# Weight remainders made by Pool instead of Vector during an expert sort, and a third buffer for stored activations

## Chip, cores and metric

The kernel runs on one core of a Trainium2 chip. The metric is the device time of one execution in microseconds; the median of the runs is given. The engines are called by the names of the profile: PE (TensorE matmul), PEld (its weight loads), DVE (VectorE), ACT (ScalarE), POOL (GpSimd) and SP (SyncE, which here only issues transfers). A name with a q behind it (SPq, ACTq) is the engine's queue, where its transfers are issued.

## What is computed

Two transformer-like blocks on 512 tokens of width 1024, all in float32: an SSD and gated-linear-attention mixer, a latent-attention layer, two gated feed-forward layers, an HGRN2 and retention mixer, and last a PEER layer (product-key experts), then a final norm. The change is in the PEER layer, with one exception at the very end:

```python
def peer_ffn(h, w_q, sub_keys, expert_u, expert_v):
    q = (ht @ w_q).reshape(T, 8, 2, 128)
    s = jnp.einsum('thpd,hpkd->thpk', q, sub_keys) 
    top_s, top_i = lax.top_k(s, 16)
    cand = top_s[:, :, 0, :, None] + top_s[:, :, 1, None, :]
    best_s, best_c = lax.top_k(cand.reshape(T, 8, 256), 16)
    ...
    gates = jax.nn.softmax(best_s, axis=-1)
    act = jax.nn.gelu(jnp.einsum('td,thkd->thk', xb, expert_u[expert_idx]))
    return jnp.einsum('thk,thkd->td', gates * act, expert_v[expert_idx])
```

## The kernel before

**Products.** A float32 matmul is made of three in a faster format: each operand is split into a high part (ACT casts it, `whi` for weights) and a remainder (`lo = src - hi`, `wlo`), and `mm3` adds hi x hi, hi x lo and lo x hi in PSUM. The weights come as a fixed stream of blocks of 128 x 1024 (0.524 MB each). `weight(name)` hands out the next block and first sees to it that the blocks behind it are loaded (`_issue`, on SP's queue) and split (`_prep`, which calls `split`, line 329). The remainder is made on DVE at line 334, like all other remainders. In the PEER layer there are four buffers each for the raw block, `whi` and `wlo`.

**The PEER layer** treats its four token tiles in two ways. For the first three tiles (384 tokens) all 16384 experts are computed densely: u blocks (128 experts each, `u`, 24 matmuls of 384 columns) give activations, v blocks (`v`, 18 matmuls of 512 columns) add weighted rows of `expert_v` into six PSUM banks. For the last tile the 128 chosen rows of `expert_u` and of `expert_v` for each token are gathered from DRAM by indirect transfers on POOL (`fetch`, line 1659, six row buffers) and treated on DVE (lines 1671 and 1678); this is the generator `rows`.

The order in time is:

1. 16 blocks of `w_pq` (queries), each followed by the scores against the keys; then u blocks 0 to 71, whose activations are stored to DRAM (`ad`, in pairs, lines 1477 and 1479). This is `main`. Into it the generator `side` is woven: first the sort of the scores (`topk`, `top16` from line 1685, on DVE alone) for eight heads, then the softmax (`soft`), then eight empty steps, then `gates`, which builds for the three dense tiles the gate of every expert by one-hot products (lines 1772 to 1790) and writes them to DRAM (`gd`, line 1756). `rows` is woven in beside it. How many steps of `side` and of `rows` are made per block of `main` is set by the numbers around line 1529.
2. What is left of the u blocks, with rows at 0.5 a block.
3. 56 steps, n = 0 to 55, of a u block (72 to 127) and the v block of the same experts: `weigh` multiplies activations by gates (line 1582), which `load_g` has read back from `gd` (line 1558), and splits the product; `v_block` adds. 2.8 rows a step.
4. 72 steps with the v blocks 0 to 71, whose activations `load_a` reads back from `ad` (line 1562, two buffers of two blocks each); rows at a rate that finishes them three steps before the end. The last step adds the result into `x`, and `final` (line 1801) normalizes and writes out through tiles `fy`.

Each engine executes its instructions in the order that the framework's scheduler has given them, which is not always that of the source: loads whose buffers are free are moved up. The layer's normalized input is made tile by tile before it starts (`norm_scale`, half of each product on POOL at line 417), with one buffer `xn`, from which PE transposes it.

Of the kernel before, what the change touches and what calls it, by code (L numbers as in the profile page):

```python
# [139 lines left out]
class Net:  # L140
    def __init__(self, ctx, tc, ap, start=None):
        self.ctx, self.tc, self.nc, self.ap = ctx, tc, tc.nc, ap
        nc = self.nc
        pool = lambda name, bufs=1, **kw: ctx.enter_context(tc.tile_pool(name=name, bufs=bufs, **kw))
        self.cp = pool("cp")
        self.raw = pool("raw", 3)
        self.whi = pool("whi", 3)
        self.wlo = pool("wlo", 3)
        self.big = pool("big", 2)
        self.sm = pool("sm", 4)  # L150
        self.xd = pool("xdram", space=DRAM).tile([P, D], F32, name="xd")
        self.pacc = pool("pacc", 4, space=PSUM)
        self.psm = pool("psm", 4, space=PSUM)
        self.stream = stream_plan()
        self.wpos = 0
        self.wload = 0
        self.wready = 0
        self.wq = []
        self.more = None
        if start is not None:  # L160
            while self.stream[self.wpos][0] != start:
                self.wpos += 1
            self.wload = self.wready = self.wpos
        self.x = self.cp.tile([P, NT, D], F32, name="x")
        self.cst = self.cp.tile([P, NCST], F32, name="cst")
        self.vec = self.cp.tile([P, NVEC], F32, name="vec")
        self.ones = self.cp.tile([P, P], F32, name="ones")
        self.eps = self.cp.tile([P, 1], F32, name="eps")
        self.dummy = self.cp.tile([P, 1], F32, name="dummy")
        self.nwp = self.cp  # L170
        self.norm = 0
        self.sq = {}
        self.nT = None
        self.identb = self.cp.tile([P, P], BF16, name="identb")
        self.negb = self.cp.tile([P, 2, P], BF16, name="negb")
        self.id3 = self.cp.tile([P, 16], BF16, name="id3")
        nc.vector.memset(self.eps, EPS)
        nc.sync.dma_start(self.x[:, 0, :512], ap["x"][0:P, :512])
        nc.sync.dma_start(self.x[:, 0, 512:], ap["x"][0:P, 512:])
        self.load_norm()  # L180
        nc.sync.dma_start(self.x[:, 1], ap["x"][P:2 * P, :])
        nc.sync.dma_start(self.cst[:, :P], ap["cst"][:, :P])
        nc.sync.dma_start(self.x[:, 2], ap["x"][2 * P:3 * P, :])
        nc.sync.dma_start(self.x[:, 3], ap["x"][3 * P:4 * P, :])
        nc.scalar.activation(self.dummy, self.eps, AF.Sqrt)
        self.ident = self.c("ident")
        self._prep()
        self._prep()
# [41 lines left out]
    def _prep(self):  # L230
# [10 lines left out]
            return  # L241
        hi = self.wbuf(self.whi, self.wready).tile([P, WB], F32R, name="whi")
        lo = self.wbuf(self.wlo, self.wready).tile([P, WB], F32R, name="wlo")
        self.split(hi[:, :n], lo[:, :n], r[:, :n])
        self.wq[self.wready - self.wpos] = (hi, lo)
        self.wready += 1

# [78 lines left out]
                    if len(grp) == 2 or tt % 2:  # L326
                        yield

    def split(self, hi, lo, src, scale=None):

        nc = self.nc
        if scale is None:
            nc.scalar.copy(hi, src)  # L333
            nc.vector.tensor_tensor(lo, src, hi.bitcast(F32), ALU.subtract)  # L334
        else:
            nc.scalar.activation(hi, src, AF.Copy, scale=scale)
            nc.vector.scalar_tensor_tensor(lo, src, scale, hi.bitcast(F32), ALU.mult, ALU.subtract)
# [1108 lines left out]
    def peer(self, last=False):  # L1446
# [4 lines left out]
        with ExitStack() as es:  # L1451
# [5 lines left out]
            with ExitStack() as e1:  # L1457
# [63 lines left out]
                    nc.scalar.copy(sc[c].rearrange("p a b -> p (a b)"), p)  # L1521

                main = itertools.chain(self.formA("w_pq", 16, hh, hl, ev_q, lead=2), experts())
                next(main)
                acc = accr = 0.0
                fin = False
                for _ in main:
                    if self.heads < 9:
                        acc += 1.7
                        if self.heads:  # L1530
                            accr += 0.3
                    else:
                        acc += 1.3
                        accr += 0.5
                    while acc >= 1:
                        acc -= 1
                        if next(side, "end") == "end":
# [20 lines left out]
                        nc.sync.dma_start(g[:, a:b], gd[a:b, :, j * 32:(j + 8) * 32].rearrange("g p c -> p g c"))  # L1558

                def load_a(j):  # L1560
                    as_[j] = pv.tile([P, 2, TD], F32, name="a")
                    nc.sync.dma_start(as_[j], ad[j // 2])

                def u_block():
# [48 lines left out]

                load_g(0, 0, 4 * ND)
                for _ in main:
                    step(0.5)
                out = [[(self.accb if nb else self.smb)() for nb in range(2)] for tt in range(ND)]
                ups = [self.accb(), self.smb()]
                au = [u_block(), u_block()]
                for n in range(P - NS):  # L1620
                    w = weigh(n, au.pop(0))
                    if n + 2 < P - NS:
                        au.append(u_block())
                    if n + 4 - (P - NS) in (0, 2):
                        load_a(n + 4 - (P - NS))
                    v_block([n], [w])
                    step(2.8)
                rate = (2 * P - self.fetched) / (NS - 3)
                for n in range(P - NS, P):
                    j = order[n]  # L1630
                    w2 = weigh(n, as_[j - j % 2][:, j % 2])
                    if j % 2 and j + 3 < NS:
                        load_a(j + 3)
                    if n < P - 2:
                        v_block([n], [w2])
                        step(rate)
# [164 lines left out]
    def final(self, fp):  # L1801
# [4 lines left out]
        def tile_out(tt):  # L1806
            r = self.x_rstd(tt)
            for i in range(2):
                s = slice(i * 512, (i + 1) * 512)
                y = fp.tile([P, 512], F32, name="fy", bufs=3)  # L1810
                nc.vector.scalar_tensor_tensor(y, self.x[:, tt, s], r, fw[:, s], ALU.mult, ALU.mult)
                (nc.sync, nc.scalar)[i].dma_start(ap["y"][tt * P:(tt + 1) * P, s], y)

# [167 lines left out]
```

## Time and profile before

| | us |
|---|---|
| median of 3 runs | 3522.71 (3520.72 to 3525.72) |
| profiled execution | 3522.2 |
| its span, first to last instruction | 3520.4 |
| PE busy | 3453.3 |
| DVE busy | 2171.0 |
| POOL busy | 520.8 |

The granted clock of TensorE was 0.995 of full speed over the span. A group of instructions is shown as line, engine, operation, output and inputs by the program's names, shapes, count, busy time and mean duration; behind the bar stands the engine's idle time just before them and what ended it. In windows, each engine's busy time stands with its number of instructions, then the granted clock (1.00 is full speed), the mean busy share of the 16 DMA engines and the GB/s that they moved.

### The profile page before, as it was taken

How to read it: one execution, taken by the hardware profiler on the slowest of the kernel's cores; microseconds unless marked ns; L12 is line 12 of the kernel's file. 1: busy time of each engine (PE TensorE's matmuls, PEld its weight loads, DVE VectorE, ACT ScalarE, POOL GpSimd, SP SyncE). 2: the span in 40 equal slices, each digit the busy share in tenths (PEclk: the TensorE clock that was granted, in tenths of full speed). 3: DMA queues.
4: the chain of work that ended last, by engine and by line, in shares of the span. 5: the costliest groups of instructions: out<-in, count | busy, mean ns of one | idle time of the engine just before them, and what ended most of it. 6: DMA issues, size and time to landing. Idle time of an engine off the chain costs nothing.

```text
span 3520.4 us, 46078 instructions
## 1 busy us (share of the span) xinstructions
PE 3453.3 (98%) x17601; PEld 2934.9 (83%) x17601; DVE 2171.0 (62%) x4070; ACT 1363.4 (39%) x2246; POOL 520.8 (15%) x403
## 2 busy tenths in 40 slices
PE   8999999999999999999999999899999999999999
PEld 7887788888778888888888888789899999997887
DVE  4455643335753333488634343599998778888887
ACT  5345432225843222545323333333444333333333
POOL 1001100000000000122101000210111354443220
PEclk9999999999999999999999999999999999999999
DMA  3221222322113332312232222435688999999996
GB/s 134 72 90 66 72 90 96 100 92 79 47 37 96 96 97 95 100 66 63 85 117 81 87 90 91 142 122 168 220 311 305 335 334 323 328 335 335 342 353 213
DMA packets 178303, 555.12 MB, mean 158 GB/s; under 512 B 19169, under 2 KB 44897, under 8 KB 177954
## 3 DMA queue, kind: packets, MB, share of 16 engines
q1 hardware_dynamic: 122944, 365.94, 31.0%
q0 software_dynamic: 36864, 134.23, 10.8%
q10 hardware_dynamic: 18274, 52.00, 3.9%
q8 instruction: 138, 2.26, 0.3%
q14 instruction: 83, 0.68, 0.1%
HBM read 508.07 MB, written 44.04 MB: 157 GB/s over the span
## 4 chain that ended last, share of the span: by engine, by line
PE 88%; DVE 7%; DMA 2%; ACT 1%; issue 1%; POOL 1%; SPq 0%; ACTq 0%; POOLq 0%; DVEq 0%
PE acc L262 22%; PE acc L263 22%; PE acc L264 22%; PE smb L264 4%; PE smb L263 4%; PE smb L262 4%; DVE wlo L334 1%; PE smb L1307 1%; PE smb L1028 1%; DMA a<-ad 1%; PE acc L996 1%; PE smb L1787 1%; PE smb L1788 1%; PE smb L1016 1%; PE smb L1424 0%
## 5 line engine op out<-in xcount | busy, mean ns | idle before, releaser
L334 DVE TENSOR_TENSOR wlo<-raw,whi 128x1024 fp32r<-128x1024 f32 (+2 forms) x621 | 761.0, 1227 | 653.2 <-ACT whi L333 629.0
L333 ACT CAST whi<-raw 128x1024 fp32r<-128x1024 f32 (+2 forms) x621 | 644.4, 1040 | 1258.1 <-PE acc L263 567.9
L264 PE MATMUL acc<-big_hi,wlo 128*128 128x512 f32 (+2 forms) x2504 | 918.1, 367 | 8.0 <-DVE wlo L334 7.7
L262 PE MATMUL acc<-big_hi,whi 128*128 128x512 f32 (+2 forms) x2504 | 923.0, 369 | 0.7 <-ACT big_hi L333 0.4
L263 PE MATMUL acc<-big_lo,whi 128*128 128x512 f32 (+2 forms) x2504 | 918.6, 367 | 1.2 <-DVE big_lo L334 1.1
L264 PEld LDWEIGHTS acc<-big_hi,wlo 128*128 128x128 f32 x2504 | 474.9, 190 | 72.2 <-DVE wlo L334 13.2
L262 PEld LDWEIGHTS acc<-big_hi,whi 128*128 128x128 f32 x2504 | 475.1, 190 | 61.8 <-ACT big_hi L333 1.0
L263 PEld LDWEIGHTS acc<-big_lo,whi 128*128 128x128 f32 x2504 | 475.5, 190 | 60.5 <-DVE big_lo L334 2.1
L262 PE MATMUL acc<-whi,big_hi 128*128 128x512 f32 x768 | 311.6, 406 | 2.3 <-DVE yret L1198 1.5
L263 PE MATMUL acc<-wlo,big_hi 128*128 128x512 f32 x768 | 300.9, 392 | 0.9 <-DVE wlo L334 0.9
L264 PE MATMUL acc<-whi,big_lo 128*128 128x512 f32 x768 | 301.6, 393 | 0.0
L1659 POOL DMA_INDIRECT row<-u_rows,ix x128 | 185.8, 1451 | 559.0 <-DVE row L1671 463.2
L1659 POOL DMA_INDIRECT row<-v,ix x128 | 153.9, 1203 | 295.5 <-DVE x L1678 272.5
L417 POOL TENSOR_TENSOR xn<-x,nw 128x512 f32<-128x512 f32 x24 | 35.2, 1469 | 1060.2 <-DVE x L458 1010.2
L333 ACT CAST wh<-w 128x384 fp32r<-128x384 f32 x128 | 65.6, 513 | 323.7 <-issue 164.7
L262 PEld LDWEIGHTS acc<-whi,big_hi 128*128 128x128 f32 x768 | 144.6, 188 | 35.2 <-issue 2.5
L263 PEld LDWEIGHTS acc<-wlo,big_hi 128*128 128x128 f32 x768 | 144.7, 188 | 30.9 <-issue 1.9
L264 PEld LDWEIGHTS acc<-whi,big_lo 128*128 128x128 f32 x768 | 144.4, 188 | 30.1
L1678 DVE SCALAR_TENSOR_TENSOR x<-row,act,x 128x1024 f32<-128x1024 f32 x128 | 164.0, 1282 | 1.3
L264 PE MATMUL smb<-whi,wl 128*128 128x512 f32 x384 | 150.9, 393 | 6.0 <-DVE wl L334 6.0
L1671 DVE SCALAR_TENSOR_TENSOR row<-row,xr 128x1024 f32<-128x1024 f32 x128 | 151.6, 1220 | 0.0
L263 PE MATMUL smb<-wlo,wh 128*128 128x512 f32 x384 | 150.4, 392 | 0.0
(525 smaller groups left out, 5363.6 us busy)
## 6 DMA issues: line engine op xcount, KB each, us to landing
raw<-u SPq DMA_DIRECT2D x128, 512.0 KB, 5.6
raw<-v SPq DMA_DIRECT2D x128, 512.0 KB, 5.9
raw<-w_gu SPq DMA_DIRECT2D x88, 512.0 KB, 3.5
raw<-w_dn SPq DMA_DIRECT2D x40, 512.0 KB, 3.6
ad<-pa ACTq DMA_DIRECT2D x36, 384.0 KB, 5.1
a<-ad SPq DMA_DIRECT2D x36, 384.0 KB, 5.4
gd<-big_hi ACTq DMA_DIRECT2D x24, 512.0 KB, 6.0
gd<-big_lo ACTq DMA_DIRECT2D x24, 512.0 KB, 6.1
```

What stands on the lines that cost most here:

```text
L262: mm(out, lh, rh, start=start, stop=False)
L263: mm(out, lh, rl, start=False, stop=False)
L264: mm(out, ll, rh, start=False, stop=stop)
L333: nc.scalar.copy(hi, src)
L334: nc.vector.tensor_tensor(lo, src, hi.bitcast(F32), ALU.subtract)
L996: mm(p[:, :n - P], q[:, i * P:n], k[:, :n - P], start=True, stop=True)
L1016: nc.tensor.transpose(banks[b][:, o + (i - k) * P:o + (i - k + 1) * P], es[i][:, k * P:(k + 1) * P], self.ident)
L1028: mm(po[64 * e:64 * e + 64, k * P:], vn[:, k, h + e], ts[e][k][:, :T - k * P], start=(k == 0), stop=(k == NT - 1))
L1307: mm(pa[:, tt - i], kx[:, tt], qx[:, tt], start=True, stop=True)
L1659: nc.gpsimd.indirect_dma_start(out=g, out_offset=None, in_=src, in_offset=bass.IndirectOffsetOnAxis(ap=ix[:, i, k:k + 1], axis=0))
L1671: pin(v.scalar_tensor_tensor(g, g, 1.0, xn, ALU.mult, ALU.mult, accum_out=act[:, k:k + 1]))
L1678: pin(v.scalar_tensor_tensor(x, g, act[:, k:k + 1], x, ALU.mult, ALU.add))
```

## The change

Between the PEER layer's first product and the end of the softmax, the remainders of weight blocks are made on POOL instead of DVE; no rows are fetched in that time, and 1.5 steps of the sort are asked for per block in place of 1.7. After it, rows are taken at 0.4 a block instead of 0.5 while the gates are made, and at 1.5 a block after them. The tile for stored activations has three buffers instead of two, and its loads are issued two blocks earlier; the output tile `fy` has two instead of three.

```diff
@@ __init__
+        self.sub = self.nc.vector
@@ _prep
-        self.split(hi[:, :n], lo[:, :n], r[:, :n])
+        self.split(hi[:, :n], lo[:, :n], r[:, :n], sub=self.sub)
@@ split
-    def split(self, hi, lo, src, scale=None):
+    def split(self, hi, lo, src, scale=None, sub=None):
...
             nc.scalar.copy(hi, src)
-            nc.vector.tensor_tensor(lo, src, hi.bitcast(F32), ALU.subtract)
+            (sub or nc.vector).tensor_tensor(lo, src, hi.bitcast(F32), ALU.subtract)
@@ peer
                 main = itertools.chain(self.formA("w_pq", 16, hh, hl, ev_q, lead=2), experts())
+                self.sub = nc.gpsimd
                 next(main)
                 acc = accr = 0.0
                 fin = False
                 for _ in main:
+                    if self.heads == 9:
+                        self.sub = nc.vector
                     if self.heads < 9:
-                        acc += 1.7
-                        if self.heads:
-                            accr += 0.3
+                        acc += 1.5
                     else:
                         acc += 1.3
-                        accr += 0.5
+                        accr += 0.4
...
                 def load_a(j):
-                    as_[j] = pv.tile([P, 2, TD], F32, name="a")
+                    as_[j] = pv.tile([P, 2, TD], F32, name="a", bufs=3)
                     nc.sync.dma_start(as_[j], ad[j // 2])
...
                 load_g(0, 0, 4 * ND)
                 for _ in main:
-                    step(0.5)
+                    step(1.5)
...
-                    if n + 4 - (P - NS) in (0, 2):
-                        load_a(n + 4 - (P - NS))
+                    if n + 8 - (P - NS) in (0, 2, 4):
+                        load_a(n + 8 - (P - NS))
...
-                    if j % 2 and j + 3 < NS:
-                        load_a(j + 3)
+                    if j % 2 and j + 5 < NS:
+                        load_a(j + 5)
@@ final
-                y = fp.tile([P, 512], F32, name="fy", bufs=3)
+                y = fp.tile([P, 512], F32, name="fy", bufs=2)
```

The order of instructions on three engines shows where things now stand (line numbers of the changed program are one or two higher).

POOL, from the end of the mixer into the PEER layer, before (`mt` belongs to the mixer, `xn` to the input's norm):

```order
L1169 TENSOR_TENSOR kr<-kr,rt 128x512
L1244 TENSOR_TENSOR mt<-mt,yret 128x512 x8
L417 TENSOR_TENSOR xn<-x,nw 128x512 x4
L1659 DMA row<-u_rows,ix 128x1024 x128
L1659 DMA row<-v,ix 128x1024 x128
```

and now:

```order
L1245 TENSOR_TENSOR mt<-mt,yret 128x512 x8
L335 TENSOR_TENSOR wlo<-raw,whi 128x1024
L418 TENSOR_TENSOR xn<-x,nw 128x512 x2
L335 TENSOR_TENSOR wlo<-raw,whi 128x1024
L418 TENSOR_TENSOR xn<-x,nw 128x512
L335 TENSOR_TENSOR wlo<-raw,whi 128x1024
L418 TENSOR_TENSOR xn<-x,nw 128x512
L335 TENSOR_TENSOR wlo<-raw,whi 128x1024 x4
L1661 DMA row<-u_rows,ix 128x1024 x2
L335 TENSOR_TENSOR wlo<-raw,whi 128x1024
L1661 DMA row<-u_rows,ix 128x1024 x4
L335 TENSOR_TENSOR wlo<-raw,whi 128x1024 x39
```

47 remainders stand on POOL, three of them ahead of an `xn`, and the first six row fetches stand between them.

ACT, at the end of the gates, before (`COPY big_lo` takes the last gates out of PSUM, `gd` is their write to DRAM, `pa` the activations of a u block that is stored, `af` those of a u block that is used at once):

```order
L1790 COPY big_lo<-smb 128x128x4
L1756 DMA gd<-big_lo 128x1024 x4
L1477 ACTIVATE pa<-acc 128x384 x2
L333 CAST whi<-raw 128x1024
L1479 DMA ad_16896<-pa 128x768
L333 CAST whi<-raw 128x1024
L1477 ACTIVATE pa<-acc 128x384
L1674 ACTIVATE act<-act 128x16
L333 CAST whi<-raw 128x1024 x2
L1477 ACTIVATE pa<-acc 128x384
L1479 DMA ad_16897<-pa 128x768
```

and now:

```order
L1792 COPY big_lo<-smb 128x128x4 x2
L1758 DMA gd<-big_lo 128x1024 x4
L1478 ACTIVATE pa<-acc 128x384
L334 CAST whi<-raw 128x1024
L1480 DMA ad_16898<-pa 128x768
L1574 ACTIVATE af<-acc 128x384
L334 CAST whi<-raw 128x1024 x2
L1574 ACTIVATE af<-smb 128x384
L334 CAST wh<-w 128x384
L334 CAST whi<-raw 128x1024
L1574 ACTIVATE af<-acc 128x384
```

Six `pa` followed the last gate write before the first `af` (four of them are shown); now one does. On PE, 216 matmuls of u blocks stood between the last gate product and the first product of a v block, and now 98.

SP, the loads around the same place, before (`a` is a pair of stored activations, `big_hi` and `big_lo` receive gates of eight blocks each):

```order
L226 DMA raw<-u 128x1024 x72
L1562 DMA a<-ad_16863 128x768
L226 DMA raw<-u 128x1024 x2
L1562 DMA a<-ad_16864 128x768
L1558 DMA big_lo<-gd 128x2x256 x4
L1558 DMA big_hi<-gd 128x12x256
L226 DMA raw<-u 128x1024
L226 DMA raw<-v 128x1024
```

and now:

```order
L227 DMA raw<-v 128x1024
L1564 DMA a<-ad_16863 128x768
L1564 DMA a<-ad_16864 128x768
L227 DMA raw<-u 128x1024
L1564 DMA a<-ad_16865 128x768
L1560 DMA big_lo<-gd 128x2x256 x4
L1560 DMA big_hi<-gd 128x12x256
L227 DMA raw<-v 128x1024
```

Three pairs of activations are loaded there instead of two, and v blocks already stand ahead of the gate reads. The next load of a pair comes when the first of these buffers is free, in the last stage.

## Rows read from the trace of the kernel before

**Rows 1.** The page's first part: busy time, share of the span, instructions.

```profile
PE 3453.3 (98%) x17601; PEld 2934.9 (83%) x17601; DVE 2171.0 (62%) x4070; ACT 1363.4 (39%) x2246; POOL 520.8 (15%) x403
```

**Rows 2.** Windows: busy PE, PEld, DVE, ACT, POOL (count), PEclk, DMA, GB/s.

```profile
2400.00:2500.00 100.00, 92.37 (x508) 87.07 (x506) 99.90 (x454) 33.28 (x45) 6.41 (x5) 1.00 0.55 177
...
3200.00:3300.00 100.00, 94.01 (x406) 77.07 (x405) 80.96 (x95) 32.55 (x44) 29.20 (x27) 0.97 0.96 349
```

**Rows 3.** Timeline of PE in u blocks; a window of v blocks.

```profile
2724.25 0.34 PE L262 MATMUL acc<-big_hi,whi 128*128 128x384 f32 x1
...
2729.45 0.33 PE L262 MATMUL acc<-big_hi,whi 128*128 128x384 f32 x1
...
3400.00:3500.00 100.00, 100.00 (x443) 82.81 (x442) 83.01 (x98) 37.32 (x53) 15.92 (x17) 1.00 0.79 281
```

**Rows 4.** Groups by line, DVE from 2298 to 2505, PE from 2400 to 2500.

```profile
L334 DVE TENSOR_TENSOR wlo<-raw,whi 128x1024 fp32r<-128x1024 f32 x38 | 46.2, 1215 | 0.0
...
L1671 DVE SCALAR_TENSOR_TENSOR row<-row,xr 128x1024 f32<-128x1024 f32 x10 | 12.1, 1214 | 0.0
...
L264 PE MATMUL acc<-big_hi,wlo 128*128 128x384 f32 x169 | 58.4, 346 | 6.1 <-DVE wlo L334 5.9
```

**Rows 5.** POOL products, lines 1167 and 1169; DVE's timeline beside them.

```profile
L1167 POOL TENSOR_TENSOR qr<-qr,ru 128x512 f32<-128x512 f32 x4 | 5.2, 1295 | 238.9 <-DVE ru L1166 213.2 <-ACT whi L333 25.7
...
L1169 POOL TENSOR_TENSOR qr<-qr,rt x4: 2262/2272/2281, 1742.8 to 2013.2; 128x512 f32<-128x512 f32 x4
...
1741.93 2.03 DVE L334 TENSOR_TENSOR wlo<-raw,whi 128x1024 fp32r<-128x1024 f32 x1
```

**Rows 6.** Timeline of POOL and ACT before the PEER layer: start, duration.

```profile
2268.31 1.27 POOL L417 TENSOR_TENSOR xn<-x,nw 128x512 f32<-128x512 f32 x1 [1.81 <-PE smb L434]
2273.48 1.28 POOL L417 TENSOR_TENSOR xn<-x,nw 128x512 f32<-128x512 f32 x1 [3.90 <-PE smb L434]
...
2267.82 1.98 ACT L333 CAST whi<-raw 128x1024 fp32r<-128x1024 f32 x2
```

**Rows 7.** Timelines and SP's waits after the gates; a window of 4 us.

```profile
2719.98 0.22 PE L1788 MATMUL smb<-o,oi 128*128 128x128 f16 x1
...
2733.85 0.36 SPq L1558 DMA_DIRECT2D big_hi<-gd  x1
...
SPq L1558 <- DMA big_hi<-gd: 7.1, 1, 7.1
...
2747.85 0.38 SPq L1558 DMA_DIRECT2D big_lo<-gd  x1
...
2758.13 0.39 PE L262 MATMUL smb<-whi,wh 128*128 128x512 f32 x1
...
2748.00:2752.00 4.00, 4.00 (x25) 4.00 (x25) 1.69 (x2) 2.77 (x4) 0.00 (x0) 1.00 1.03 391
```

**Rows 8.** The chain, timelines and windows where the last stage begins.

```profile
3213.74 13.75 DMA a<-ad
...
3227.59 0.56 DVE L1582 SCALAR_TENSOR_TENSOR w<-a,big_lo 128x384 f32<-128x384 f32 x1 [7.34 <-DMA a<-ad]
...
3229.81 0.80 PE L264 MATMUL smb<-whi,wl 128*128 128x512 f32 x1 [5.99 <-DVE wl L334]
...
3200.00:3220.00 20.00, 19.99 (x88) 16.26 (x87) 20.00 (x23) 6.18 (x8) 13.13 (x10) 1.00 0.97 363
3220.00:3240.00 20.00, 14.02 (x55) 11.09 (x54) 11.02 (x15) 5.07 (x8) 3.43 (x4) 0.83 0.94 337
```

**Rows 9.** DMA queues from 3240 to 3470; a window of 4 us with a backlog.

```profile
DMA packets 31446, 80.34 MB, mean 349 GB/s; under 512 B 2894, under 2 KB 13646, under 8 KB 31430
...
3220.00:3224.00 4.00, 3.82 (x17) 2.81 (x15) 0.25 (x1) 1.46 (x2) 1.01 (x1) 1.00 1.04 397
```

**Rows 10.** The end: DVE's timeline; DMA issues, KB each, us to landing.

```profile
3516.65 0.75 DVE L1811 SCALAR_TENSOR_TENSOR fy<-x,nr,nw 128x512 f32<-128x512 f32 x1 [0.57 <-DMA y<-fy]
...
y<-fy SPq DMA_DIRECT2D x4, 256.0 KB, 2.0
```

## The prediction

> **What bounds the kernel.** The page's first part comes first: TensorE (PE) is busy for 98% of the span [rows 1], so a change can only give back the stretches in which PE does less than its pace, or add to them. The windows of 100 us show where these are: from 2300 on PE is near 100 in all but 2400 to 2500, where VectorE (DVE) is full, and 3200 to 3300 [rows 2]. Busy time hides part of a loss, since matmuls overlap, so I go by pace: from the first to the last of 31 PE rows of u blocks (384 columns) it is (2729.45 - 2724.25) / 30 = 0.1733 us each, 24 x 0.1733 = 4.16 us a block; of a v block (512 columns) a full window holds 443, 0.2257 us each, 18 x 0.2257 = 4.06 us a block [rows 3]. With that, 508 matmuls in 2400 to 2500 are 88.0 us of work: 12.0 us were lost, of which 7.6 us are visible idle time [rows 2]. And 88 + 55 matmuls in 3200 to 3240 are 32.3 us: 7.7 us lost [rows 8].
>
> **Sort, taken off DVE.** In 2298 to 2505 DVE does 38 remainders (`wlo`, 46.2 us) and 10 rows (12.1 us) beside the sort, without a gap, and PE waits at line 264 for `wlo` [rows 4]. The change takes both away: some 58 of 207 us. It also asks for 1.5 instead of 1.7 side steps per block, so the sort is spread over 5 more u blocks, 47 remainders on GpSimd (Pool) instead. What the sort keeps, 207 - 46 - 12 = 149 us, is due only when DVE next has to make a `wlo`: by then PE has done 14 pq blocks of 24 x 0.2257 = 5.4 us and 31 u blocks of 4.16, 205 us. There is room of some 55 us, and that is what hides Pool's effect on DVE, below; without it PE would wait for the sort's end at the first gate block. Gain: 12.0 us, at least the visible 7.6. I take 12.
>
> **Price of a remainder on Pool.** No row shows Pool on 128x1024 with two full inputs. Rows of 128x512 take 1.29 us, and 2.27 us where they met a `wlo` of DVE [rows 5], so a remainder is bounded by 2.5 and 4.5 us. A u block leaves 4.16 us. Line 1169 is the row of 2.27: its first starts at 1742.8, while a DVE `wlo` runs, which itself took 2.03 us [rows 5] and not 46.2 / 38 = 1.22 [rows 4]. So the two engines exclude each other there, and each lost about a microsecond. I take 2.5 to 3.2 us, since in the sort most DVE instructions are short and have one tensor as input; then Pool keeps pace and nothing of it lies on the path. The sort's two-input parts are held up by Pool in the same way, at most some 20 times by a microsecond or two, within the room above.
>
> **Pool's queue, moved past.** The order puts remainders between the `xn` products that normalize the PEER input. Before, the third `xn` starts at 2268.31 and the fourth at 2273.48 [rows 6]. Now a remainder goes ahead of the third; its `whi` is one of two casts that start at 2267.82 [rows 6], so it runs from about 2268.9 to 2271.4, `xn` to 2272.7, the next remainder to 2275.2, and the fourth `xn` starts 1.7 us later than it did, on the path to the transposes. Bounds: 0 (the DVE remainders that left that place give time back) and 4 us (locked). I take 2. Six row fetches also stand among the remainders of blocks 8 and 9 and wait for head 0's indices; Pool has over 2 us to spare in each pq block of 5.4 us, so this is nearly covered: 0.5.
>
> **End of the gates: a new wait.** The first v block needs gates for all tokens, read back from DRAM after the last gate block is written. Before: last gate matmul 2719.98, the read of 1.5 MB issued at 2733.85, landed at 2747.85 when the sync queue that waited for it goes on; the first v matmul ran at 2758.13 [rows 7]. The chain of 27.7 us was hidden, because nine u blocks (37 us) followed the gates on PE. In the new order the gates end five blocks later and four u blocks (98 matmuls, 17.0 us) follow. The chain then needs 27.7 plus 1.2 us (weigh and cast), less 17.0: PE would wait 11.9 us. The transfers on the way are bound by bandwidth (391 GB/s there, [rows 7]), and the order has two writes of `ad` and one raw block fewer there and a third `a` more: about 1.0 MB net, and probably a row, so 3 to 4 us sooner. I take a wait of 8.5 us, and 2.5 us for a slow clock after it: after the gap at 3224 the granted clock is 0.83 in that window, between the two levels, and 7.7 us were lost for some 6 of waiting [rows 8]. Cost 11. Ends: 0 (the chain with its own 4.7 MB alone takes 12 us of transfer and 3 of copies, under 17) and 14.5.
>
> **Three activation buffers.** The weighing at 3227.59 waited 7.34 us for `a`, whose load, issued only at 3213.74, three blocks ahead, took 13.75 us [rows 8]. Now three pairs are loaded at the gates' end and a load runs five blocks ahead, 20 us. Gain 7.5 of the 7.7.
>
> **Rows, moved to the end.** What the sort no longer fetches comes later: by the order DVE adds 84 v rows after the 56 u-and-v blocks where it added 68, 1.2 a block instead of 0.97. For DVE this is 0.23 x 1.21 us (a row's price, [rows 4]) more in a block of 4.06 us in which it was 83% busy [rows 3]: covered. For the transfers, 16 rows of 0.524 MB are 8.4 MB over 70 blocks (285 us), 29 GB/s on top of 349 [rows 9]: 378. Whether that fits is not shown by a mean in which nothing waited. Bounds: 0, as stretches with a backlog move 397 [rows 9], and 285 x (378/349 - 1) = 24 us, if 349 were all there is. The 397 is the nearer row, same stage and same mix, so I take 2.5 for peaks in the blocks that also load gates.
>
> The Trainium skill's SBUF — State Buffer, section Summary: rules for kernel authors, says to reckon with about 358 GB/s from HBM; the windows with a backlog go above it. By that figure the last stage would cost 285 x (378/358 - 1) = 16 us.
>
> **Output tiles.** With two `fy` buffers the last two outputs wait for transfers two tiles back rather than three. The last already waited 0.57 us; an output takes 2.0 us to land [rows 10]. Cost 0.7.
>
> **Sum** against the profiled execution's 3522.2 us: -12 + 2 + 0.5 + 11 - 7.5 + 2.5 + 0.7 = -2.8, so 3519.4; the median of the runs stands 0.5 higher, at 3522.71, hence 3520. A measurement of this kernel can tell about 0.2%, 7 us, from no change.
>
> **Rivals.**
> First, the gate chain is short enough. If fewer transfers share the bandwidth while PE still has 17 us of work, the wait falls to 2 us or less and the sum to 3510. For it: all bytes between 2720 and 2748 moved at a saturated 391 GB/s, so bytes removed are time removed. Against: the last of the four gate writes and the read queue behind other transfers, and that is unchanged. 0.28.
>
> Second, on the slower side: the last stage becomes bound by transfers. Place: the v blocks after 3230. It decides if the sustained rate is below the 378 needed; 16 us at 358, up to 24 at 349, in place of 2.5. The time would be 3533 to 3541. For it: the stage already moved 349 with a DMA share near full. Against: 397 with a backlog in that stage. By the page's 358 it would be so; the windows speak against it. 0.13.
>
> Third, Pool does not keep pace. If a remainder costs the upper 4.5 us, each u block in the sort takes 4.5 instead of 4.16: 29 x 0.34 = 10 us, and the gain of 12 shrinks to 2: 3530. For it: the 2.27 rows. Against: these met a long DVE instruction each; here DVE's are mostly 0.3 us. 0.09.
>
> Fourth, the change does not reach PE: the sort's loss was only the visible 7.6 us and the buffer's part is replaced by a late raw block. Then 3527 or so, no measurable difference. 0.05.
>
> **Chances.** The forecast proper holds 0.45, and spreads from 3513 to 3528 by the bounds of the gate wait and of the last stage: most of it within 0.2%, a little faster. Faster: 0.28 + 0.05 = 0.33. Slower: 0.13 + 0.07 (most of the third) + 0.01 = 0.21. Same: the rest, 0.46. The range must hold the first rival and the lower part of the second: 3507 to 3536; the forecast's own is 3513 to 3528.
>
> **What would show it.** In the changed profile: no PE wait for `wlo` in the sort, and windows there with 115 matmuls per 20 us; Pool's remainder row at 2.5 to 3.2 us; a PE wait of some 8 us at the first v block, behind the weighing, which waits for the gate read; no wait for `a` at the v stage; pace of v blocks 0.226 us after it. The prediction is wrong if the first v block waits little, if v blocks lose pace or wait for raw blocks or rows in the last 280 us, or if Pool's row is above 4.16 us.

## The result: 0.87% slower, in one pause of PE

The changed kernel takes 3553.30 us (median of 4 runs, 3552.06 to 3553.97) against 3522.43 for the kernel before on the same chip: ratio 1.0087, 95% interval 1.0075 to 1.0099. The prediction said 3520 in a range of 3507 to 3536. The profiled execution's span went from 3520.4 to 3551.0 us.

### The profile page after: what moved, and what is told of

It is laid out like the page before. It is cut to its first block, busy times and chain, and to the rows that moved or that the text cites. A ratio compares the mean times of both kernels' runs of the same rounds, so it can differ in the third digit from the quotient of the medians.

```text
span 3551.0 us, 46094 instructions
## 1 busy us (share of the span) xinstructions
PE 3456.2 (97%) x17601; PEld 2939.5 (83%) x17601; DVE 2152.2 (61%) x4023; ACT 1362.5 (38%) x2246; POOL 641.9 (18%) x450
## 4 chain that ended last, share of the span: by engine, by line
PE 91%; DVE 3%; issue 2%; DMA 2%; POOL 1%; ACT 1%; DVEq 0%; ACTq 0%; POOLq 0%; SPq 0%
PE acc L263 24%; PE acc L264 23%; PE acc L265 23%; PE smb L265 4%; PE smb L264 4%; PE smb L263 4%; PE smb L1308 1%; PE smb L1029 1%; PE acc L997 1%; PE smb L1789 1%; PE smb L1790 1%; DMA raw<-v 1%; PE smb L1017 1%; DVE wlo L335 1%; PE smb L1425 0%
## 5 line engine op out<-in xcount | busy, mean ns | idle before, releaser
L335 DVE TENSOR_TENSOR wlo<-raw,whi 128x1024 fp32r<-128x1024 f32 (+1 forms) x574 | 704.2, 1228 | 709.0 <-ACT whi L334 683.8
L334 ACT CAST whi<-raw 128x1024 fp32r<-128x1024 f32 (+2 forms) x621 | 644.1, 1039 | 1267.0 <-PE acc L264 568.1
L263 PE MATMUL acc<-big_hi,whi 128*128 128x512 f32 (+2 forms) x2504 | 924.1, 369 | 31.9 <-ACT whi L334 30.2
L1661 POOL DMA_INDIRECT row<-v,ix x128 | 162.0, 1265 | 242.6 <-DVE x L1680 219.6
L334 ACT CAST wh<-w 128x384 fp32r<-128x384 f32 x128 | 65.6, 513 | 313.6 <-PE acc L264 138.8
L263 PE MATMUL smb<-whi,wh 128*128 128x512 f32 x384 | 150.7, 392 | 7.1 <-ACT wh L334 7.1
```

The costliest lines, as they stand in the source:

```text
L263: mm(out, lh, rh, start=start, stop=False)
L335: (sub or nc.vector).tensor_tensor(lo, src, hi.bitcast(F32), ALU.subtract)
L1661: nc.gpsimd.indirect_dma_start(out=g, out_offset=None, in_=src, in_offset=bass.IndirectOffsetOnAxis(ap=ix[:, i, k:k + 1], axis=0))
```

## The profile after

In the changed kernel lines are one higher than before up to 334, and one or two higher behind: the split's cast is L334, its subtraction L335, the exp of the softmax L1745. The page's busy part [rows 1]:

```profile
PE 3456.2 (97%) x17601; PEld 2939.5 (83%) x17601; DVE 2152.2 (61%) x4023; ACT 1362.5 (38%) x2246; POOL 641.9 (18%) x450
```
The windows of the two stretches of [rows 2], with the same columns:

```profile
2400.00:2500.00 100.00, 68.34 (x377) 67.51 (x376) 88.21 (x383) 24.78 (x34) 38.65 (x16) 0.83 0.34 114
...
3200.00:3300.00 100.00, 97.36 (x442) 82.15 (x441) 87.00 (x97) 34.01 (x46) 43.92 (x35) 0.98 0.97 358
```

The busy part says little; the windows say where. In 2400 to 2500 PE does 377 matmuls where it did 508, and now DVE too has idle time there. Smaller windows show one hole:

```profile
2420.00:2440.00 20.00, 20.00 (x118) 20.00 (x117) 19.93 (x104) 5.20 (x7) 7.18 (x3) 1.00 0.37 125
2440.00:2460.00 20.00, 4.66 (x27) 4.34 (x26) 19.93 (x123) 0.00 (x0) 0.00 (x0) 0.71 0.00 0
2460.00:2480.00 20.00, 3.67 (x10) 3.17 (x11) 19.90 (x87) 7.43 (x10) 5.12 (x3) 0.50 0.17 63
2480.00:2500.00 20.00, 20.00 (x110) 20.00 (x110) 8.45 (x9) 5.75 (x8) 14.01 (x6) 0.94 0.65 219
```

The waits of that stretch (engine, line, what it waited for, us in total, times, longest):

```profile
PE acc L263 <- ACT whi L334: 30.2, 1, 30.2
...
ACT gt L1745 <- DVE gt L1744: 40.8, 1, 40.8
```

Everything stops but DVE: ACT, Pool and the transfers show 0 in 2440 to 2460. PE waits for a cast of ACT, and ACT waits for DVE. ACT's timeline (start, duration, what ended the idle time before) names the instruction at the head of its queue:

```profile
2428.88 0.48 ACT L1478 ACTIVATE pa<-acc 128x384 f32<-128x384 f32 x1
2429.38 1.28 ACT L1745 ACT_TABLE_LOAD   x1
2471.44 0.63 ACT L1745 ACTIVATE gt<-gt 128x512 f32<-128x512 f32 x1 [40.77 <-DVE gt L1744]
...
2473.76 1.98 ACT L334 CAST whi<-raw 128x1024 fp32r<-128x1024 f32 x2
```

It is the exp of the softmax, which needs the sort's last result, `gt` less its maximum (L1744), and that starts only at 2470.72 on DVE. ACT works in order, so the casts behind the exp wait too; without casts there are no remainders (called low parts from here on), no matmuls, and no raw block's buffer comes free. Before, the same exp stood behind 22 u blocks' activations and waited from 2485.07 to 2495.04; now it stands behind 10, and gets its turn at 2430.67. In the kernel before, its row on ACT was:

```profile
2495.04 0.63 ACT L1743 ACTIVATE gt<-gt 128x512 f32<-128x512 f32 x1 [9.97 <-DVE gt L1742]
```

To see what each stretch gave, I take PE's landmarks from its timelines and subtract the u matmuls of each stretch at the pace of 0.1733 us [rows 3]. The rest, in us:

| stretch | before | after | change | predicted |
|---|---|---|---|---|
| start to first u matmul (2382.40, 2385.19) | | | +2.8 | +2.5 |
| to first gate matmul (2524.72, 2570.65), less 740 and 860 u | 14.1 | 36.4 | **+22.3** | **-12** |
| gates (to 2719.98, 2765.95), u not subtracted | 195.3 | 195.3 | 0 | 0 |
| to first v matmul (2758.13, 2789.83), less 216 and 98 u | 0.7 | 6.9 | +6.2 | +8.5 |
| to last u matmul (3198.21, 3231.22), less 1272 and 1270 u | 219.6 | 221.3 | +1.7 | +2.5 |
| to last matmul (3512.59, 3542.42) | 314.4 | 311.2 | -3.2 | -5.0 |
| to the span's end | 7.8 | 8.6 | +0.8 | +0.7 |

The changes add up to 30.6, the difference of the two spans. All but the sort's row come to 8.3 where the prediction had 9.2. One profile of each kernel stands behind the table. The first row is the least certain: the seven kernels of this document that share the changed kernel's start reach the first u matmul between 2383.09 and 2386.40.

Pool's timeline at the norm, which answers to [rows 6]:

```profile
2267.28 1.81 POOL L418 TENSOR_TENSOR xn<-x,nw 128x512 f32<-128x512 f32 x1 [4.36 <-PE smb L435]
2271.52 2.34 POOL L335 TENSOR_TENSOR wlo<-raw,whi 128x1024 fp32r<-128x1024 f32 x1 [2.43 <-ACT whi L334]
2273.82 1.72 POOL L418 TENSOR_TENSOR xn<-x,nw 128x512 f32<-128x512 f32 x1
2275.50 2.35 POOL L335 TENSOR_TENSOR wlo<-raw,whi 128x1024 fp32r<-128x1024 f32 x1
2277.81 1.29 POOL L418 TENSOR_TENSOR xn<-x,nw 128x512 f32<-128x512 f32 x1
```
The low parts now stand between the `xn` products. At the gates' end [rows 7], the wait of the weighing for the gate read:

```profile
DVE w L1584 <- DMA big_hi<-gd: 4.3, 1, 4.3
```

and PE's timeline at the first v matmul:

```profile
2789.83 0.80 PE L263 MATMUL smb<-whi,wh 128*128 128x512 f32 x1 [5.04 <-ACT wh L334]
```

A window where the last stage begins [rows 8]:

```profile
3240.00:3260.00 20.00, 17.36 (x74) 13.36 (x74) 16.51 (x20) 7.04 (x9) 11.33 (x7) 1.00 1.03 393
```

The transfers from 3260 to 3500 [rows 9]:

```profile
DMA packets 34621, 91.61 MB, mean 382 GB/s; under 512 B 3248, under 2 KB 14000, under 8 KB 34602
```

DVE's timeline at the last output [rows 10]:

```profile
3546.58 1.41 DVE L1813 SCALAR_TENSOR_TENSOR fy<-x,nr,nw 128x512 f32<-128x512 f32 x2 [1.44 <-DMA y<-fy]
```

The first v block does wait for the gate read, PE for 5.04 us instead of the 8.5 expected. The weighing of the last stage no longer waits for `a`, but PE does only 74 v matmuls in 3240 to 3260 (a full window of 20 us holds 443 / 5, some 89 [rows 3]): a block of raw v weights, issued at 3245.11, lands 13.77 us later. From 3260 to 3500 the transfers move 382 GB/s in the mean.

## The experiments

All ratios are to the kernel before, run beside each kernel on the same chip; its median on these chips was 3522.69 to 3523.33. A name such as e7 in an expectation means the experiment that has it in its heading.

**The exp held back, in the changed kernel.**

```diff
-        nc.scalar.activation(g, g, AF.Exp)
+        self.tc.keep_in_program_order(nc.scalar.activation(g, g, AF.Exp))
```

> The changed kernel with one edit: the softmax's exp is held behind everything that the program gives ScalarE (ACT) before it, so it stands behind 29 u blocks instead of 10. Theory A (ACT works in order, its exp waits 40.8 us for the sort, and the casts of the weights behind it with it): the 34.5 us that PE lost in 2440 to 2500 come back, 3553.3 - 34.5 = about 3519, PE at pace (115 matmuls per 20 us) to the gates, the sort still ends near 2471 and ACT waits there for nothing. Rival B (Pool's remainders or the raw loads are what starves PE): 3545 or more, with a PE wait for low parts left in the sort. Rival C (the loss lies in the gates' read-back and the last stage): no change, 3550 to 3555.

Measured: 3519.06 us, ratio 0.9986 (0.9977 to 0.9995). PE is at pace, as the window of this kernel shows:

```profile
2400.00:2500.00 100.00, 100.00 (x579) 100.00 (x578) 99.76 (x381) 34.69 (x49) 59.15 (x24) 1.00 0.53 174
```

From the first u block to the first gate it loses 1.4 us instead of 36.4. So the exp's place in ACT's queue costs the 34 us; with the exp held back the change ends at 3519, where the prediction had 3520. One thing went otherwise than expected: the sort ended not near 2471 but with its last subtraction at 2490.82, as Pool went on making low parts beside it. The exp, at 2510.67, still did not wait.

**The same edit in the kernel before.** The diff is the same.

> The kernel before with the same one edit: its exp moves from behind 22 u blocks to behind 24, some 9 us later. Theory A: of its wait of 10.0 us at most 3 are left (the sort ends some 2 us later, since VectorE now has two more low parts to make first), 5 of the 5.8 us that PE lost in 2480 to 2500 come back: 3517 to 3519. Theory as in the prediction (the loss in 2400 to 2500 is VectorE being late with low parts, wherever the exp stands): 3521 to 3524.

Measured: 3522.56 us, ratio 1.0002 (0.9993 to 1.0011). The exp's wait fell from 10.0 to 1.4 us and PE gained nothing (a window of this kernel; PE at pace does 115):

```profile
2480.00:2500.00 20.00, 16.41 (x77) 15.70 (x77) 20.00 (x87) 7.51 (x9) 1.68 (x1) 0.83 0.44 151
```

Here theory A missed and the prediction's reading of the loss held: in the kernel before PE is short because DVE is late with low parts, and the exp's wait lies beside that. This is why the wait could be overlooked: it stood in the trace at 9.97 us and cost nothing there.

**Pool alone, in the kernel before**: the changed kernel with rates, row fetches, activation and output buffers put back (a piece of the edit).

```diff
-                        acc += 1.5
+                        acc += 1.7
+                        if self.heads:
+                            accr += 0.3
```

> The kernel before with one part of the change: Pool makes the low parts during the sort; rates, row fetches and activation buffers stay as they were. The exp then stands behind 12 u blocks (before: 22) without being touched. Theory A (Pool holds up VectorE's sort, and the exp, which has come forward, waits for it on ACT): the sort has its 177 us and 12 rows of 1.22 us, ends near 2486, ACT reaches the exp near 2435 and waits some 50 us, PE loses about 44 us: 3553 to 3560, the whole of the change's loss and more, with no wait at the first v block. Rival (the slower sort rate or the rows moved are what costs): 3515 to 3530.

Measured: 3558.82 us, ratio 1.0100 (1.0085 to 1.0116). The number came as expected, the way to it only in part. The waits of this kernel, 2380 to 2530:

```profile
PE acc L265 <- POOL wlo L335: 28.2, 6, 8.4
...
ACT gt L1747 <- DVE gt L1746: 19.8, 1, 19.8
```

and a piece of Pool's timeline:

```profile
2450.03 0.95 POOL L1663 DMA_INDIRECT row<-u_rows,ix  x1 [11.47 <-DVE tv L1692]
2451.01 9.36 POOL L335 TENSOR_TENSOR wlo<-raw,whi 128x1024 fp32r<-128x1024 f32 x4
```

The exp waits 19.8 us, not 50. The larger part is Pool's own queue: a row fetch waits 11.5 us for a row buffer that DVE, busy sorting, has not given back, and four low parts are queued behind it. The change's "no rows fetched then" takes just this away, and leaves the exp's wait at its full length.

**Three buffers alone, in the kernel before**: the changed kernel without Pool's part and with the old rates (a piece of the edit).

```diff
-                self.sub = nc.gpsimd
...
-                    if self.heads == 9:
-                        self.sub = nc.vector
```

> The kernel before with another part alone: three buffers of stored activations, loaded earlier, and two output tiles. As the prediction has it, 7.5 us of wait for the activations go and 0.7 come at the end: 3515 to 3517. By the traces of the changed kernel (the stretch from the last u block to the end is 3.2 us shorter, and a block of raw v weights is late there in place of the activations): 3518 to 3521. Rival: nothing, 3522 to 3524.

Measured: 3515.88 us, ratio 0.9979 (0.9970 to 0.9988). That is the prediction's term (-7.5 and +0.7): 7.4 us less than before's 3523.32. My later guess from the changed kernel's trace, 3518 to 3521, was wrong: what is missing there is lost to something else, below. The last stage runs at pace from its start; its windows, where [rows 8] had 55 matmuls in the second:

```profile
3200.00:3220.00 20.00, 20.00 (x88) 16.21 (x87) 20.00 (x22) 6.49 (x9) 13.55 (x10) 1.00 0.97 350
3220.00:3240.00 20.00, 20.00 (x89) 16.52 (x88) 16.79 (x23) 7.53 (x10) 5.52 (x5) 1.00 1.03 403
```

**Low parts left to ACT's copies, exp held back (e7)**: Pool is taken out of the sort and DVE given nothing for it.

```diff
-            (sub or nc.vector).tensor_tensor(lo, src, hi.bitcast(F32), ALU.subtract)
+            if sub is nc.gpsimd:
+                nc.scalar.copy(lo, src)
+            else:
+                nc.vector.tensor_tensor(lo, src, hi.bitcast(F32), ALU.subtract)
```

> The changed kernel with the exp held back, and in the sort the low parts' subtraction left out: ACT copies the weights there in its place, so neither Pool nor VectorE makes low parts (the result is not the reference's). It measures what Pool does to the sort. Theory A (an instruction of Pool with two inputs holds up certain instructions of VectorE until it ends): the sort takes its own 149 us, from 2295 to about 2446, and the rows of eq 128x512, bi 128x64 and cb 128x64 fall from 829, 654 and 849 ns back to 421, 186 and 302. Rival (the sort is slow for another reason in the changed program): it ends near 2472 and the rows stay. The time itself is about that with Pool, 3516 to 3521, as PE was at pace there already.

Measured: 3510.52 us, ratio 0.9965 (0.9952 to 0.9978). The sort runs from 2287.81 to the subtraction at 2440.60, 152.8 us; with Pool beside it throughout (the exp held back) it runs from 2294.75 to 2490.82, 196.1 us. The last subtraction with Pool beside it, then without:

```profile
2490.82 0.68 DVE L1744 TENSOR_TENSOR gt<-gt,tm 128x512 f32<-128x512 f32 x1
...
2440.60 0.68 DVE L1747 TENSOR_TENSOR gt<-gt,tm 128x512 f32<-128x512 f32 x1
```

Three groups of DVE in the sort (line, engine, operation, count, busy us, mean ns), first of the changed kernel:

```profile
L1715 DVE TENSOR_SCALAR bi<-bi 128x64 uint32<-128x64 uint32 x16 | 9.8, 654 | 0.0
...
L1723 DVE TENSOR_TENSOR cb<-bi,cf 128x64 bf16<-128x64 uint32 x8 | 6.8, 849 | 0.0
...
L1691 DVE FIND_INDEX8 tix<-tv,big_lo 128x8 uint32<-128x128 f32 x32 | 9.1, 284 | 0.0
```

and of this one, without Pool:

```profile
L1718 DVE TENSOR_SCALAR bi<-bi 128x64 uint32<-128x64 uint32 x16 | 2.3, 184 | 0.0
...
L1726 DVE TENSOR_TENSOR cb<-bi,cf 128x64 bf16<-128x64 uint32 x8 | 2.4, 299 | 0.0
...
L1694 DVE FIND_INDEX8 tix<-tv,big_lo 128x8 uint32<-128x128 f32 x32 | 9.1, 285 | 0.0
```

So Pool does hold DVE: short arithmetic such as these two groups is stretched, the index searches are not. By the timelines of both engines in the changed kernel up to 2432, five of the six pairs of L1715 start while a low part runs on Pool; they take 1.79 us in the mean and each ends within 0.3 us of it, and the sixth takes 0.28. One of the five: in the changed kernel's timeline of Pool a low part runs from 2429.05 to 2431.44,

```profile
2429.05 2.39 POOL L335 TENSOR_TENSOR wlo<-raw,whi 128x1024 fp32r<-128x1024 f32 x1 [1.76 <-ACT whi L334]
```

and in DVE's the pair of instructions that met it (0.37 us in all without Pool, by the group above) ends at 2431.59:

```profile
2429.32 2.27 DVE L1715 TENSOR_SCALAR bi<-bi 128x64 uint32<-128x64 uint32 x2
```

The time itself fell 8.5 us below that with Pool, which I had not expected: the first u matmul is at 2377.72 instead of 2386.17, so all of it lies in the norm and the pq blocks.

**The same with the exp free**, as the changed kernel places it.

```diff
-        self.tc.keep_in_program_order(nc.scalar.activation(g, g, AF.Exp))
+        nc.scalar.activation(g, g, AF.Exp)
```

> As e7 (in the sort ACT copies the weights where the low parts would be made; their subtraction is left out), but with the exp where the changed kernel has it, behind 10 u blocks. It parts the 40.8 us that the exp waited into what Pool's hold on VectorE made and what the exp's early place makes alone. Theory A: without Pool the sort ends near 2441, ACT comes to the exp near 2420 and waits about 20 us, PE stands still for about 10 and loses 13 to 15 in all against e7: 3522 to 3526; so of the 35 us that the exp costs in the changed kernel some 20 are Pool's. Rival (the early place alone makes it all): 3535 or more. Rival (Pool's hold makes it all): 3510 to 3513.

Measured: 3522.70 us, ratio 0.9998 (0.9988 to 1.0007). The exp waits 17.26 us:

```profile
2441.30 0.63 ACT L1748 ACTIVATE gt<-gt 128x512 f32<-128x512 f32 x1 [17.26 <-DVE gt L1747]
```

PE loses 11.4 us between the first u block and the first gate, against 1.4 with the exp held back and 36.4 with Pool. The early place alone makes 10 of the 35 us. The other 25 need both: Pool's hold makes the sort end later, but with the exp held back that costs PE nothing (1.4 us with Pool and without).

**The exp held back, DVE makes the low parts**: what Pool is worth.

```diff
-                self.sub = nc.gpsimd
...
-                    if self.heads == 9:
-                        self.sub = nc.vector
```

> The changed kernel with the exp held back and the low parts in the sort made by VectorE again: what Pool is worth once the exp is out of the way. The sort would end near 2502 (149 us of its own and some 45 low parts of 1.22 us), before the exp, which stands near 2505. Theory A: PE loses only what late low parts cost, 5 us as between 2400 and 2480 of the kernel before, and the norm does not wait for Pool (2.8 us back): 3520 to 3523, against 3519 with Pool. If VectorE has to be freed for PE to keep pace: 3530 or more.

Measured: 3525.66 us, ratio 1.0007 (0.9998 to 1.0016), a little above the expectation. By its profile PE loses 9.7 us in the sort against 1.4 with Pool, and reaches the first u block 5.3 us sooner. So Pool is worth 6.6 us by the medians (3525.66 - 3519.06), once the exp is out of the way; the two profiled executions are only 2.4 us apart (spans of 3520.5 and 3518.1), as this kernel's profiled run, 3522.3, was among its fastest. The sort itself ended sooner than expected: it runs from 2289.48 to its last subtraction at 2479.39, 189.9 us with 33 low parts (39.8 us) in it. That is less than the 196.1 with Pool: Pool does not make the sort shorter.

**The gates' read-back**: the exp held back and the old rate of 1.7, so that nine u blocks follow the gates again.

```diff
-                        acc += 1.5
+                        acc += 1.7
```

> The changed kernel with the exp held back and the sort's rate put back from 1.5 to 1.7 side steps a block, so that about nine u blocks instead of four follow the gates; the exp stands behind 24 u blocks, near 2487, later than the sort's end at 2471. Theory A, with the price of the gates' read-back as the trace gives it (6.2 us of wait and 1.3 after it): 3553.3 - 34.5 - 7.5 = about 3511, no PE wait at the first v block. If the read-back's wait is only moved (the first v block waits for something else): 3518 to 3520, as without the rate.

Measured: 3516.27 us, ratio 0.9981 (0.9972 to 0.9990), between the two expectations. PE still loses 10.3 us before the first v block, now because a block of raw u weights is late: the sync queue, which also issues the gate read and waits there for the gates' last write, issues it only at 2732.42 and it lands 14.70 us later. What was gained lies behind: the stretch from the last u block to the end is 307.1 us instead of 311.7.

**Activation loads kept back as well (e8)**, against the last kernel:

```diff
-                    nc.sync.dma_start(as_[j], ad[j // 2])
+                    self.tc.keep_in_program_order(nc.sync.dma_start(as_[j], ad[j // 2]))
```

> The changed kernel with the exp held back, 1.7 side steps a block, and the loads of stored activations kept behind what the program gives the sync queue before them, so that the first three go out after the u-and-v blocks are nearly done and not between the gates' last write and their read-back. If the 10.3 us lost before the first v block at 1.7 come from transfers that stand in the way there (three loads of 0.39 MB at 391 GB/s are 3.0 us): 3 to 7 us less, 3509 to 3513. Rival (the raw u block is late because the sync queue waits for the gates' write, whatever else is loaded): no change, 3515 to 3517.

Measured: 3512.27 us, ratio 0.9969 (0.9957 to 0.9981). The loss before the first v block falls from 10.3 to 5.8, but the intervals of this kernel and the last overlap. The cause was found two kernels on.

**Rows fetched earlier (e10)**, against the last kernel:

```diff
-                    step(2.8)
+                    step(3.1)
```

> e8 with the rows fetched somewhat faster beside the u-and-v blocks, 3.1 instead of 2.8 a block, so that about 67 rows instead of 84 are left for the last 72 blocks, as in the kernel before. If the rows moved to the end are what makes a block of raw v weights late after the last u block (the stretch from the last u block to the end was 308.8 us in e8, 311.2 in the changed kernel, 306.5 with three buffers alone): that stretch falls to 306 to 307 and the time by 2 to 3 us, 3509 to 3511. Rival (the block is late because its load is issued late, whatever else is loaded): the stretch stays at 308 to 311, the time at 3512 or more.

Measured: 3514.60 us, ratio 0.9971 (0.9961 to 0.9982). The stretch behind the last u block is 310.8 us, not 306 to 307. DVE adds 66 rows after the last u block, against 82 in the last kernel, so the number of rows left for the last stage is not what makes its raw block late; the rival held.

**The first gate read on Pool's queue (e11)**, against the last kernel:

```diff
-                load_g(0, 0, 4 * ND)
+                load_g(0, 0, 4 * ND, nc.gpsimd)
```

> e10 with the first read of the gates issued by Pool's queue instead of the sync queue, which waits for the gates' last write and holds the raw u blocks behind it. If that order is what costs the 5.8 us left before the first v block in e8: they fall to 2 or less, 3505 to 3508. Rival (the transfers themselves are late, bound by 390 GB/s): no change against e10.

Measured: 3508.55 us, ratio 0.9960 (0.9946 to 0.9973). The loss before the first v block is 0.1 us: it was the order on the sync queue, not the bandwidth. The intervals of this kernel and the last overlap; the loss is read from one profile of each.

**The other gate reads kept in order**, on the sync queue:

```diff
-                        e.dma_start(g[:, a:b], gd...
+                        (e and e.dma_start or pin)(g[:, a:b], gd...
```

> e11 with the rows back at 2.8 a block and each pair of gate reads kept where the program has it on the sync queue, so that they are spread over six blocks and six of them (1.6 MB) no longer go out together ahead of two blocks of raw v weights, as the changed kernel has it just after the last u block. If that bunch is what makes a block of raw v weights late there (the stretch from the last u block to the end is 308.4 us in e11): 306 to 307 and 3505 to 3508. Rival (the backlog of transfers there is the same whatever their order): 308 to 311, and 3508 to 3512.

(`e` is the queue given for the first read, `pin` is `keep_in_program_order`; against the last kernel, with the rows back at 2.8.) Measured: 3504.24 us, ratio 0.9948 (0.9934 to 0.9961). The stretch behind the last u block falls from 308.4 to 306.3 us, and from 2300 to 3490 the waits list none of PE's. (The rate of the rows has no part in it: 308.8 us at 2.8 in the kernel with activation loads kept back.) The sync queue's timeline after the last u block, in the kernel before this one:

```profile
3193.21 3.47 SPq L1560 DMA_DIRECT2D big_hi<-gd  x6
3197.21 6.04 SPq L227 DMA_DIRECT2D raw<-v  x2
```

and in this one, with the reads kept in order:

```profile
3191.89 0.89 SPq L1556 DMA_DIRECT2D big_hi<-gd  x2
3195.89 0.34 SPq L227 DMA_DIRECT2D raw<-v  x1
3196.28 0.53 SPq L1556 DMA_DIRECT2D big_hi<-gd  x1
```

In the kernel before this one, six gate reads went out together ahead of the raw v blocks. That order is not enough by itself to make them late: with the rate of 1.7 and the activation loads not kept back, the same six reads went out at 3200.13 and two raw v blocks at 3204.32, and the stretch was 307.1 us. There the v blocks were issued 8.4 us after the last u matmul, in the changed kernel 10.6. What sets that difference is not shown, and the 2.1 us are read from one profile of each kernel.

This last kernel, with Pool's low parts, three buffers, the exp and the loads held in place and the first gate read on Pool's queue, is the fastest of all, 0.5% below the kernel before, though its interval overlaps the last one's.

## Why the prediction was wrong

- **The step that failed** is in the part on the sort: what the sort keeps "is due only when DVE next has to make a `wlo`", hence "room of some 55 us". The sort is due sooner, when ACT comes to the softmax's exp, which stands among the casts. By the changed order that is after 10 u blocks (2430.67), not after 31, so there was no room but a lack of 40.8 us. The prediction looked at DVE and Pool in that stretch and not at ACT, where the exp comes forward past a dozen u blocks' casts.
- **The gain of 12 us was real.** With the exp held back PE loses 1.4 us there instead of 14.1, a gain of 12.7. With the low parts on DVE and all else the same 9.7 us are left, so Pool makes 8.3 of the gain; the rest came with the rows left out and the slower sort, as holding back the exp alone gave nothing. That the exp held back brings the time to 3519, close to the 3520, is not luck in the main: by the table's rows that kernel's terms are +3.8, -12.7, 0, +6.9, +1.5, -2.6 and +0.8, each within 2.4 us of the predicted one. Only the last stage's is near for the wrong reason (below).
- **Pool's hold on DVE** was named ("some 20 times by a microsecond or two"): it was 196.1 - 152.8 = 43 us over 39 low parts, somewhat more than this makes. A sort of 196 us would still have fitted the 205 of the supposed room; the error was the room. In the changed kernel, with the exp early, 25 of the 35 us come with it. The 149 us that "the sort keeps" hold only without Pool (152.8 measured). The Trainium skill's SBUF — State Buffer, section Who interferes with whom, states an exclusive hold for the whole instruction where DVE has two SBUF inputs while GpSimd reads SBUF, or where DVE is in a two-port mode, which `tensor_scalar` can enter; the rows of L1715 and L1723 agree, though none shows whether L1715 was in such a mode. The index searches keep their 284 ns.
- **A low part on Pool**: 2.5 to 3.2 us taken, 2.44 measured between 2294 and 2432 (25 of them). Pool kept pace, and the third rival falls. The fourth falls by the 12.7 us; its other half, a late raw block in place of the buffers' gain, came in part.
- **The norm**: 2.5 taken, 2.8 measured, and only in part for the reason given. From the first `xn` product to the fourth it is 16.2 us (2261.63 to 2277.81) instead of 14.4 (2259.05 to 2273.48): 1.75 for the low parts in Pool's queue, where 2 was taken. But the first product itself is 2.6 us later: already in the blocks ahead of the norm PE waits 2.1 us for a low part of DVE's, before 0.9. The pq blocks then give 1.5 back. The size is not settled: this landmark varies by 3 us between kernels with the same start, and the two kernels with the exp held back that differ only in Pool are 5.3 us apart there.
- **The gates' read-back**: 8.5 + 2.5 taken, 6.2 + 1.7 measured, inside the range given. (The chain of 27.7 us is 27.9 by its own rows.) The first rival (2 us or less) did not come.
- **Three buffers**: -7.5 and +0.7 taken together, 7.4 us less alone. In the changed kernel only 3.2 of it is seen in the last stage. The 4.7 us between its 311.2 and the 306.5 of the buffers alone are the raw v block, and there the prediction's term (2.5 for moved rows) had the wrong cause: fewer rows left in the last stage did not shorten it (310.8 with 66, 308.8 with 82). The rate of 1.7 brought the stretch to 307.1, spreading the gate reads to 306.3; why the block is late in the changed kernel and hardly with that rate stays open.
- **Rival 2**, the last stage bound by transfers, falls: they move 382 GB/s as a mean over 240 us, and from 3280 on PE does 90 matmuls in every 20 us, its pace.

## What to carry to other kernels

Where a scheduler sets the order, taking work off an engine can bring the readers of its results forward in other engines' queues: the exp stood behind 22 u blocks with the low parts on DVE and behind 10 to 12 without them, whatever the chip then needed. So for each result of the engine concerned, look up on every in-order queue where its first reader stands and what is queued behind it; the time from there to the result's real end is the price. Work handed to Pool is not simply off DVE: here a low part on Pool held DVE's short arithmetic to its end, though not the searches. Count what it holds up, and put the reader of DVE's result where it can wait without harm.

## What the runs showed of the hardware

Pool's product of 128x1024 with two inputs took 2.39 us undisturbed (at 2429.05), and cost the sort beside it 43 / 39 = 1.1 us each, nearly what DVE needs to make a low part itself, 1.22 [rows 4]; with DVE making them the sort took 189.9 us, with Pool 196.1. What Pool saves here is thus not DVE's time but PE's wait: the low part comes on time while DVE is held, and PE loses 1.4 us in the sort instead of 9.7.

The pause in the changed kernel cost PE more than its waits: it waited 30.2 us for the cast and 1.5 for a low part, but in 2440 to 2500 it did 147 matmuls, 25.5 us of work at pace, and so lost 34.5. After it had stood still, PE's granted clock was 0.50 in 2460 to 2480, the lower of its two levels (1.2 of 2.4 GHz), and 0.94 in the next window.
